# Low parts of weight units: one subtraction in four moved from VectorE to an adding transfer

## The chip, the cores and the metric

The kernel runs on one core of one Trainium2 chip. A core has a matrix engine (PE in the profile, with its weight loads as PEld), a vector engine (DVE), a scalar engine (ACT), a general engine (POOL), and a queue that does nothing here but start transfers (SP). The profile counts 16 DMA engines that carry the transfers. The metric is the device time of one execution in microseconds, as a median of several runs.

## The reference, cut to what matters

The reference is a two-layer decoder trunk over 256 tokens of width 1024. Layer 0 normalises the rows and projects them through one wide input matrix into the columns of a sparse attention, a block attention and a cross-attention into 256 memory tokens. It gates the three outputs and maps them through an output matrix. Layer 1 has the same layout with chunked retention (four heads) and cross-attention again. All weights are float32:

```python
for layer in range(DEPTH):
    if layer % 2 == 0:
        x = even_layer(x, mem_n, cos, sin, *layer_params[layer])
    else:
        x = odd_layer(x, mem_n, rcos, rsin, *layer_params[layer])
return rms_norm(x, final_norm_g)
...
h = rms_norm(x, norm_g)
(...) = _split(h @ w_in, ...)
...
y = jnp.concatenate([...], axis=-1) @ w_out
return x + y
```

What counts here is that almost all of the arithmetic is `h @ w_in`, `mem_n @ w_mem_kv` and `... @ w_out`, with every weight used once.

## The kernel before, in words

**Three products for one.** A float32 product is built from the shorter format float32r. Each operand is written as a sum of a high part (the value rounded to float32r) and a low part (the value minus the high part, again float32r). `mm3` (L133) adds three matmuls into one PSUM bank: high times high (L135), then two with one low part each (L136, L137). All three go into the same bank, one after the other.

**Units of weights.** The host lays the input matrices out as 23 chunks of 512 columns, one chunk of 280 columns, and 14 blocks of the output matrices. A chunk of 512 columns holds 1024 x 512 weights and is used in four units. One unit is 128 x 1024 float32 (512 KB): two of the eight row tiles. `units` (L126) is a generator that yields a chunk's four units: it takes a raw tile that a transfer on SP's queue fills (`load`, L87; tag `raw`, 6 slots), and calls `split` (L118). `split` makes the high part with a copy on ACT (L122, tile `whi`, 3 slots) and the low part with a subtraction on DVE (L123, tile `wlo`, 3 slots). The next step of whatever called `units` is the matmuls of that unit.

**Who uses units.** `project` (L139) has the tokens as stationary operand and the weights as moving operand: 12 matmuls of 128 x 512 for a unit; the first one that needs a low weight is an L136. `project_turned` (L161) has the weights as stationary operand: 24 matmuls of 128 x 256 for a unit, and the first that needs a low weight is an L137, since the operands change places. `project_mem` (L168) is a mixture of both. Chunk `nz` at the start does not go through `units` but calls `split` by half units (L257 to L259). The output projections (L641) call `split` as well, without `units`. So `units` serves 22 chunks of 512 columns (`ksw`, `nq`, `e0`, `mz`, `mk`, `m0`, `mq`, `mv`, `m1`, `e1`, `rq0`, `rk0`, `rv0`, `rz0`, `rv1`, `rz1`, `rq1`, `rk1`, `rv2`, `rz2`, `rv3`, `rz3`, in this order in the program) and the one of 280 columns (in `compress`, L445).

**The rest.** Between the projections stand the attention pieces of layer 0 (`causal_pair`, L358; `mem_attention`, L395) and the retention heads of layer 1 (`ret_head`, L728). They need PE for scores, transposes and outputs, ACT for exponentials and copies, and DVE for reductions and scalings.

**What sets the order.** The program is written in dataflow order. A planner, which plays the program against a time model of its own, gives each engine one fixed order of instructions and adds the semaphores; each queue then runs strictly in that order. Slots of a tag go round: a unit can be written into `whi` or `wlo` once the last matmul that reads the unit three places earlier has ended, and a load can be issued into `raw` once the reader of the unit six places earlier has ended. Matmuls that add into one bank stay in the program's order. POOL has only a few fills of constants before the change: L465, L467, L469 and L518 in the sparse attention's preparation.

Of the kernel before, what the change touches and what calls it, by code (L numbers as in the profile page):

```python
# [10 lines left out]
F32R = mybir.dt.float32r  # L11
I32 = mybir.dt.int32
AF = mybir.ActivationFunctionType
ALU = mybir.AluOpType
AX = mybir.AxisListType

P = 128
# [35 lines left out]
def trunk(  # L53
# [19 lines left out]
    nc = tc.nc  # L73
    sb = ctx.enter_context(tc.tile_pool(name="sb", bufs=1))
    pp = ctx.enter_context(tc.tile_pool(name="pp", bufs=4, space=bass.MemoryType.PSUM))
    V, S, G, PE = nc.vector, nc.scalar, nc.gpsimd, nc.tensor
    count = [0]

    def tl(tag, shape, bufs=1, dt=F32):
        count[0] += 1  # L80
        return sb.tile(shape, dt, tag=tag, bufs=bufs, name=f"{tag}_{count[0]}")
# [5 lines left out]
    def load(t, src):  # L87
        nc.sync.dma_start(t, src)
        return t
# [28 lines left out]
    def split(raw, cols, tag=None):  # L118

        hi = tl(tag or "whi", [P, 1024], NV if tag else 3, F32R)[:, :cols]  # L120
        lo = tl(tag or "wlo", [P, 1024], NV if tag else 3, F32R)[:, :cols]
        S.copy(hi, raw)  # L122
        V.tensor_tensor(lo, raw, hi.bitcast(F32), ALU.subtract)  # L123
        return hi, lo

    def units(src, idx, cols):  # L126

        for u in range(4):
            raw = ahead.pop(0) if ahead else load(tl("raw", [P, 1024], NRAW)[:, : 2 * cols], src[idx + u // 2][:, (u % 2) * 2 * cols : (u % 2 + 1) * 2 * cols])
            wh, wl = split(raw, 2 * cols)  # L130
            yield 2 * u, wh, wl

    def mm3(ps, lh, ll, rh, rl, start, stop, shared=False):  # L133

# [4 lines left out]
    def project(src, idx, lhs, cols=512, tag="pj"):  # L139

        hi, lo = lhs
        ps = [bank(tag) for _ in range(2)]
        for k0, wh, wl in units(src, idx, cols):
            for tok in range(2):
                for j in range(2):
                    kt = k0 + j
                    ts = slice(tok * P, (tok + 1) * P)
                    cs = slice(j * cols, (j + 1) * cols)
                    mm3(ps[tok][:, :cols], hi[:, kt, ts], lo[:, kt, ts], wh[:, cs], wl[:, cs], kt == 0, kt == KT - 1)
        return [p[:, :cols] for p in ps]  # L150
# [10 lines left out]
    def project_turned(src, idx, lhs):  # L161

        ps = [bank("pj") for _ in range(2)]
        for kt, wh, wl in units(src, idx, 512):
            turned_unit(ps, lhs, wh, wl, (kt, kt + 1), range(4))
        return ps

    def project_mem(src, idx, lhs):  # L168

        hi, lo = lhs  # L170
        ps = [bank("pj") for _ in range(2)]
        for k0, wh, wl in units(src, idx, 512):
            turned_unit(ps, lhs, wh, wl, (k0, k0 + 1), range(2))
            for tok in range(2):
                for j in range(2):
                    kt = k0 + j
                    ts = slice(tok * P, (tok + 1) * P)
                    c = slice(j * 512 + 256, j * 512 + 512)
                    mm3(ps[1][:, tok * T : (tok + 1) * T], hi[:, kt, ts], lo[:, kt, ts], wh[:, c], wl[:, c],
                        kt == 0 and tok == 0, kt == KT - 1, True)  # L180
        return ps
# [73 lines left out]
    for q in range(4):  # L255
        gain_split(xraw[q // 2], vect[:, V_G0 : V_G0 + 8], xh, xl, 4 * (q // 2), range(2 * q, 2 * q + 2))
        for j in range(2):  # L257
            wh, wl = split(wraw[q][:, j * 512 : (j + 1) * 512], 512)
# [658 lines left out]
```

## Time and profile before

| | |
|---|---|
| time, median of 3 runs | 444.86 us (444.41 to 445.07) |
| time of the profiled execution | 444.81 us |
| its span, from the first to the last instruction | 443.0 us |
| mean granted TensorE clock | 0.991 |
| instructions | 7033 |
| read from HBM | 72.73 MB |

The times in the prediction are read from one profiled execution. In a row of a group, `x124` is the count of instructions; what stands behind the bar is their busy time in us, the mean length of one in ns, and then the idle time of the engine just before them and what ended it. In a row of the waits, the numbers are the total in us, how often, and the longest. In a row of the timeline the first number is the start in us from the start of the span, the second the length. In a row by windows come the stretch, its length, and for each engine its busy time and its count of instructions, then the granted clock, the share of the DMA engines and GB/s. In a row of transfers the last number is the median time from issue to landing in us.

### The profile page before, as it was taken

The page shows a single profiled execution, that of the slowest core. Times are in us where ns is not written, and L with a number is a line of the kernel's source. Part 1 is how long each engine was busy: PE and PEld are TensorE (multiplying, and loading weights), DVE is VectorE, ACT ScalarE, POOL GpSimd, SP SyncE. Part 2 cuts the span into 40 slices and gives each one's busy share as a digit, 9 for nine tenths or more (in the row PEclk, how much of TensorE's full clock was granted, in tenths as well). Part 3 has the DMA queues.
Part 4 walks back from the last instruction along what each step waited for, and adds up shares of the span by engine and source line. Part 5 has one row for each costly group of instructions (what it writes and reads, how often), then busy time and mean ns, then how long its engine had stood idle before and what let it go on. Part 6 is the DMA issues. An engine that isn't in the chain of part 4 may idle for free.

```text
span 443.0 us, 7033 instructions
## 1 busy us (share of the span) xinstructions
PE 427.0 (96%) x2610; PEld 361.5 (82%) x2610; DVE 308.8 (70%) x712; ACT 245.7 (55%) x445; POOL 1.9 (0%) x9
## 2 busy tenths in 40 slices
PE   8999999999999799999999999999999999999991
PEld 6988999788777567669998988888998888888880
DVE  4997796996576666749668675768777586765415
ACT  5755637776657966737355443754534456445504
POOL 0000000000000000000000000000000000000000
PEclk9999999999999999999999999999999999999996
DMA  8975955753445514343453453664654545765202
GB/s 282 383 248 180 341 168 187 242 169 117 119 132 153 195 55 137 101 131 109 158 188 127 158 165 128 196 197 142 209 169 165 148 171 173 212 212 166 77 0 95
DMA packets 22226, 74.24 MB, mean 168 GB/s; under 512 B 2736, under 2 KB 3504, under 8 KB 22192
## 3 DMA queue, kind: packets, MB, share of 16 engines
q1 hardware_dynamic: 21616, 72.95, 50.1%
q10 hardware_dynamic: 576, 0.84, 0.6%
q8 instruction: 20, 0.33, 0.3%
q14 instruction: 14, 0.11, 0.1%
HBM read 72.73 MB, written 1.05 MB: 167 GB/s over the span
## 4 chain that ended last, share of the span: by engine, by line
PE 95%; DVE 2%; ACT 1%; DMA 1%; issue 0%; ACTq 0%
PE pj L135 24%; PE pj L136 24%; PE pj L137 24%; PE s L100 4%; PE t L194 4%; PE o L100 3%; PE tr L136 1%; PE s L135 1%; PE s L136 1%; PE s L137 1%; PE tr L135 1%; PE tr L137 1%; DMA vec<-in_vec 1%; PE s L732 1%; PE tr L194 1%; DVE v L800 1%
## 5 line engine op out<-in xcount | busy, mean ns | idle before, releaser
L123 DVE TENSOR_TENSOR wlo<-raw,whi 128x1024 fp32r<-128x1024 f32 (+2 forms) x124 | 145.1, 1173 | 72.8 <-ACT whi L122 71.9
L122 ACT CAST whi<-raw 128x1024 fp32r<-128x1024 f32 (+2 forms) x124 | 124.7, 1008 | 96.7 <-PE pj L137 36.8
L136 PE MATMUL pj<-wlo,big 128*128 128x512 f32 (+2 forms) x264 | 99.2, 376 | 0.0
L137 PE MATMUL pj<-whi,big 128*128 128x512 f32 (+2 forms) x264 | 98.4, 373 | 0.0
L135 PE MATMUL pj<-whi,big 128*128 128x512 f32 (+2 forms) x264 | 92.7, 376 | 0.0
L135 PE MATMUL pj<-big,whi 128*128 128x256 f32 x288 | 81.6, 287 | 0.8 <-ACT big L214 0.7
L136 PE MATMUL pj<-big,whi 128*128 128x256 f32 x288 | 81.1, 285 | 0.0
L137 PE MATMUL pj<-big,wlo 128*128 128x256 f32 x288 | 80.6, 286 | 0.0
L136 PEld LDWEIGHTS pj<-wlo,big 128*128 128x128 f32 x264 | 49.7, 188 | 9.7 <-issue 1.0
L135 PEld LDWEIGHTS pj<-big,whi 128*128 128x128 f32 x288 | 54.8, 191 | 2.6 <-ACT big L214 1.1
L137 PEld LDWEIGHTS pj<-whi,big 128*128 128x128 f32 x264 | 49.7, 188 | 8.7 <-issue 0.3
L135 PEld LDWEIGHTS pj<-whi,big 128*128 128x128 f32 x264 | 49.2, 188 | 8.0
L137 PEld LDWEIGHTS pj<-big,wlo 128*128 128x128 f32 x288 | 54.3, 191 | 1.4 <-issue 1.0
L136 PEld LDWEIGHTS pj<-big,whi 128*128 128x128 f32 x288 | 55.0, 191 | 0.4 <-DVE big L215 0.2
L367 ACT ACTIVATE p<-p,mx 128x128 f32<-128x128 f32 (+1 forms) x48 | 21.3, 447 | 3.1 <-DVE mx L365 3.1
L379 ACT COPY pt<-t 128x384 f32<-128x384 f32 x24 | 11.5, 479 | 12.7 <-PE t L194 12.6
L194 PE MATMUL t<-cst,p 128*128 128x128 f32 x104 | 17.9, 282 | 0.6 <-ACT pt L379 0.6
L365 DVE CUSTOM_DVE_ANT_0 p<-s,cst 128x128 f32<-128x128 f32 (+1 forms) x48 | 14.3, 354 | 5.2 <-PE t L194 5.1
L194 PEld LDWEIGHTS t<-cst,p 128*128 128x128 f32 x104 | 11.7, 140 | 6.1 <-issue 3.0
L123 DVE TENSOR_TENSOR v<-raw,v 128x1024 fp32r<-128x1024 f32 x4 | 4.9, 1226 | 14.7 <-PE tr L136 10.9
L135 PE MATMUL pj<-whi,y 128*128 128x512 f32 x36 | 13.4, 408 | 1.0 <-ACT y L387 1.0
L136 PE MATMUL pj<-wlo,y 128*128 128x512 f32 x36 | 14.2, 396 | 0.0
(280 smaller groups left out, 574.0 us busy)
## 6 DMA issues: line engine op xcount, KB each, us to landing
raw<-in_w SPq DMA_DIRECT2D x91, 512.0 KB, 4.0
raw<-in_wout SPq DMA_DIRECT2D x28, 512.0 KB, 3.9
v<-in_xtok SPq DMA_DIRECT2D x4, 512.0 KB, 7.6
raw<-in_w SPq DMA_DIRECT2D x4, 280.0 KB, 3.9
v<-in_w SPq DMA_DIRECT2D x2, 512.0 KB, 5.6
raw<-in_memT SPq DMA_DIRECT2D x2, 512.0 KB, 3.8
raw<-in_memtok SPq DMA_DIRECT2D x2, 512.0 KB, 4.3
v<-in_grow SPq DMA_DIRECT2D x2, 512.0 KB, 7.5
```

The lines of the kernel that those rows point to most:

```text
L100: ins = PE.matmul(out, lhs, rhs, start=start, stop=stop)
L122: S.copy(hi, raw)
L123: V.tensor_tensor(lo, raw, hi.bitcast(F32), ALU.subtract)
L135: PE.matmul(ps, lh, rh, start=start, stop=False, skip_group_check=shared)
L136: PE.matmul(ps, lh, rl, start=False, stop=False, skip_group_check=shared)
L137: PE.matmul(ps, ll, rh, start=False, stop=stop, skip_group_check=shared)
L194: PE.transpose(b[:, i * P : (i + 1) * P], a, ident)
L365: V.tensor_tensor_reduce(p[:, hh, a], ss[hh][tok], cpak[:, C_CAUSAL + a.start : C_CAUSAL + a.stop], -1.0, 3e38, ALU.add, ALU.min, mx[:, hh ...
L367: S.activation(p[:, hh, a], p[:, hh, a], AF.Exp, bias=mx[:, hh, tok : tok + 1], scale=-1.0, accum_out=sm[:, hh, tok : tok + 1])
L379: got = S.copy(pt[:, hh, :384], transposes([p[:, hh, i * P : (i + 1) * P] for i in range(3)]))
L732: PE.matmul(s[:, 0:T], k[:, d, 0:P], q[:, d], start=d == 0, stop=d == 1)
L800: V.tensor_tensor(x0[tok][:, bc], acc[tok][c0 // 512], x0[tok][:, bc], ALU.add)
```

## The change

In `units`, the third of a chunk's four units (`u == 2`) of a chunk with 512 columns gets a different split. ACT makes the high part as before. ACT also writes the negated raw weights, rounded to float32r, into `wlo`; that is the negated high part. Then a transfer, issued on POOL's queue, adds the raw weights to what stands in `wlo`. Its sum is the raw value minus the high part, the low part that DVE computed before. It concerns 22 units, one of each of the 22 chunks; the 280-column chunk, chunk `nz` and the output projections are untouched.

```diff
+    def split_dma(raw):
+
+        hi = tl("whi", [P, 1024], 3, F32R)
+        lo = tl("wlo", [P, 1024], 3, F32R)
+        S.copy(hi, raw)
+        S.activation(lo, raw, AF.Copy, scale=-1.0)
+        nc.gpsimd.dma_start(lo, raw, accum_op=ALU.add)
+        return hi, lo
+
     def units(src, idx, cols):
 
         for u in range(4):
             raw = ahead.pop(0) if ahead else load(tl("raw", [P, 1024], NRAW)[:, : 2 * cols], src[idx + u // 2][:, (u % 2) * 2 * cols : (u % 2 + 1) * 2 * cols])
-            wh, wl = split(raw, 2 * cols)
-            yield 2 * u, wh, wl
+            if u == 2 and cols == 512:
+                yield 2 * u, *split_dma(raw)
+            else:
+                yield 2 * u, *split(raw, 2 * cols)
```

## The prediction

> **What bounds the kernel now.** I read the head of the page first, then the chain that ended last, then the table by windows.
>
> ```profile
> span 443.0 us, 7033 instructions
> PE 427.0 (96%) x2610; PEld 361.5 (82%) x2610; DVE 308.8 (70%) x712; ACT 245.7 (55%) x445; POOL 1.9 (0%) x9
> ...
> PE 95%; DVE 2%; ACT 1%; DMA 1%; issue 0%; ACTq 0%
> ```
>
> PE is busy for 427.0 of 443.0 us and holds 95% of the chain. By stages (the first number behind the stretch is its length, the second PE's busy time):
>
> ```profile
> 16.00:62.00 46.00, 46.00 (x317) 41.87 (x316) 39.52 (x86) 27.57 (x38) 0.31 (x1) 1.00 0.70 251
> 62.00:196.00 134.00, 130.03 (x853) 101.14 (x849) 94.10 (x289) 90.11 (x226) 0.53 (x1) 1.00 0.47 148
> 196.00:256.00 60.00, 59.92 (x469) 56.01 (x470) 44.92 (x78) 31.48 (x56) 0.00 (x0) 1.00 0.45 149
> 256.00:382.00 126.00, 126.00 (x665) 108.30 (x665) 91.02 (x192) 61.34 (x72) 0.00 (x0) 1.00 0.54 172
> ```
>
> PE has no hole from 16 to 62 us nor from 196 to 382 us, even where DVE is busy for 39.52 of 46 us; the attention of layer 0 (62 to 196 us) leaves 3.97 us. So what can shorten the kernel is only what PE waits for. The waits say whether that is DVE:
>
> ```profile
> DVE wlo L123 <- ACT whi L122: 71.9, 65, 4.2
> ACT whi L122 <- PE pj L137: 36.8, 34, 3.2
> ...
> PE o L100 <- ACT pt L379: 1.8, 1, 1.8
> ...
> PEld pj L136 <- DVE wlo L123: 0.3, 1, 0.3
> ...
> PEld pj L137 <- DVE wlo L123: 0.2, 1, 0.2
> ```
>
> PE's weight loads waited for a low part twice, 0.5 us in all. It is the other way round: ACT's high parts wait for PE to free a slot, and DVE's low parts wait for ACT. DVE runs ahead of the bound.
>
> **What is removed.** For 22 units, one subtraction on DVE.
>
> ```profile
> L122 ACT CAST whi<-raw x124: 602/1047/1075, 4.5 to 416.6; 128x1024 fp32r<-128x1024 f32 x112, 128x512 fp32r<-128x512 f32 x8, 128x560 fp32r<-128x560 f32 x4
> L123 DVE TENSOR_TENSOR wlo<-raw,whi x124: 683/1225/1227, 5.1 to 417.7; 128x1024 fp32r<-128x1024 f32 x112, 128x512 fp32r<-128x512 f32 x8, 128x560 fp32r<-128x560 f32 x4
> ...
> L268 ACT ACTIVATE raw<-raw x2: 1060/1060/1060, 74.8 to 77.7; 128x1024 f32<-128x1024 f32 x2
> ...
> DMA to landing us min/median/max: 2.8/4.1/8.5
> ```
>
> (Durations in ns: least, median, most; the last row is of the loads into `raw`.) That is 22 x 1.225 = 27.0 us off DVE. It is worth the 0.5 us of waits above at most, and I count 0: those waits belong to any of 124 units, of which 22 change.
>
> **What is added.** Per unit, one activation on ACT and one transfer.
>
> ```profile
> L777 ACT ACTIVATE v<-pj,rstd 128x512 f32<-128x512 f32 x8 | 5.5, 688 | 8.7 <-PE pj L137 8.7
> ```
>
> The low part existed 1.05 us (ACT) plus 1.23 us (DVE) after ACT began the unit. Now it exists after two ACT passes and a landing. The nearest row for the second pass is the 128x1024 activation of L268, 1.06 us, so 2.1 us for both. The bounds are 1.0 us, since the rounding copy of the same shape takes that, and 1.4 us, if it went by twice a 128x512 activation (L777, 0.69 us).
>
> ```profile
> q1 hardware_dynamic: 21616, 72.95, 50.1%
> ```
>
> No row shows an adding transfer, nor any transfer from POOL's queue. It moves the shape of a `raw` load (128x1024 f32, 512 KB) and has to read two tiles where a load reads one. A median load lands after 4.1 us. Queue q1 kept 16 engines busy for 50.1% of 443.0 us, 222 us, to move 72.95 MB; another 0.524 MB so costs 1.6 us. I take 4.1 + 1.6 = **5.7 us**. The low end is 2.8 us, the shortest load (adding and second read free); the high end is 8.5 + 1.6 = 10.1 us, the longest load with the second read. With 2.1 us before it, the low part is there 7.8 us after ACT begins the unit, 5.5 us later than before.
>
> [...]
>
> **How much of it is hidden.** Between ACT's start on a unit and PE's first matmul with its low part lies the time that hides the new path; it cannot grow, as ACT starts when PE frees one of three slots. The first, the fifteenth and the last of the 22 units, each with ACT's start and that matmul:
>
> ```profile
> 21.68 1.05 ACT L122 CAST whi<-raw 128x1024 fp32r<-128x1024 f32 x1
> ...
> 24.98 0.39 PE L136 MATMUL s<-wlo,big 128*128 128x512 f32 x1
> ...
> 282.58 1.04 ACT L122 CAST whi<-raw 128x1024 fp32r<-128x1024 f32 x1
> ...
> 287.00 0.61 PE L135 MATMUL pj<-whi,big 128*128 128x512 f32 x2
> 287.46 0.39 PE L136 MATMUL pj<-wlo,big 128*128 128x512 f32 x1
> ...
> 369.38 1.04 ACT L122 CAST whi<-raw 128x1024 fp32r<-128x1024 f32 x1
> ...
> 375.93 0.40 PE L136 MATMUL pj<-wlo,big 128*128 128x512 f32 x1
> ```
>
> These are 3.3, 4.9 and 6.5 us. Read the same way in the timeline, the 22 units have, in program order (us): ksw 3.3, nq 6.2, e0 6.4, mz 9.3, mk 5.4, m0 11.0, mq 8.0, mv 9.3, m1 7.0, e1 5.5, rq0 7.2, rk0 7.9, rv0 7.0, rz0 6.5, rv1 4.9, rz1 6.5, rq1 5.1, rk1 6.0, rv2 7.1, rz2 6.5, rv3 4.9, rz3 6.5. What falls short of 7.8 us is a hole on PE: 4.5, 1.6, 1.4, 2.4, 0.8, 2.3, 0.6, 0.8, 1.3, 2.9, 1.3, 2.7, 1.8, 0.7, 1.3, 2.9, 1.3 = **30.6 us in 17 units**; five units (mz, m0, mq, mv, rk0) are covered. Nothing gives the time back: the next chunk's unit again waits for its slot.
>
> What PE can do meanwhile: products of high parts (L135) that do not need the low part, as many as there are banks, two for a unit. In some units both already go ahead (287.00 above, x2); for about ten the second is new, 0.23 us each, -2.3 us. In the attention stage other matmuls are ready: I take half of mk's 2.4 us off, -1.2 us.
>
> **Queues.** POOL's queue is in order and has two fills that wait long:
>
> ```profile
> 55.29 0.31 POOL L467 MEMSET yf<- 64x256 f32 x1 [53.73 <-PE o L457]
> 63.37 0.53 POOL L518 MEMSET tmp<- 128x512 f32 x1 [7.77 <-PE s L100]
> ```
>
> ```profile
> 48.92 1.04 ACT L122 CAST whi<-raw 128x1024 fp32r<-128x1024 f32 x1
> ...
> 55.25 0.40 PE L137 MATMUL pj<-big,wlo 128*128 128x256 f32 x2
> ```
>
> A transfer queued behind the first fill would not start before 55.6 us. For e0's unit (ACT starts at 48.92 us, low part needed by the second of the two L137, at 55.4 us) that is a hole of up to 5.9 us instead of 1.4, once. I count 0, as the planner places instructions by when they become ready, and e0's does some 4 us earlier. On ACT the new passes are 22 x 1.06 = 23 us, 55% to 61% busy. ACT's casts already wait for PE (36.8 us above), so in the projections they fit. The raw slot is held 5.5 us longer, and loads queued behind on SP shift with it; the cover is six slots:
>
> ```profile
> ACT whi L122 <- DMA raw<-in_w: 1.7, 2, 1.3
> ```
>
> ACT waited for loads 1.7 us in the whole kernel; without that cover each of the 22 would cost up to 5.5 us, so I keep 0. DMA engines gain 22 x 2 x 1.6 = 70 us at most of 16 engines' 443, from 50% to 66%.
>
> ```profile
> L378 DVE TENSOR_SCALAR p<-p,sm 128x128 f32<-128x128 f32 (+1 forms) x36 | 9.9, 312 | 0.4
> ```
>
> [...]
>
> **The sum**, against the profiled execution: 30.6 - 2.3 - 1.2 = +27.1 us on 444.8 us, **472 us**. The profiled 444.81 us stands 0.05 us below the median of the three runs, 444.86 us.
>
> **The rivals.**
>
> *Slow transfer.* An add costs more than a second read, or the queue's start is slow: 7 us and above. At 8.5 us the low part is there after 10.6 us, 21 units fall short, by 86 us; with -5 us for L135 that is +81 us, 526 us. Then PE's holes also meet the clock that is granted to it:
>
> ```profile
> 432.97 0.28 PE L137 MATMUL s<-v,y 128*128 128x256 f32 x1
> ```
>
> ```profile
> 431.60:435.10 3.50, 1.65 (x10) 1.22 (x8) 3.22 (x6) 1.98 (x7) 0.00 (x0) 1.00 0.00 0
> 435.20:441.00 5.80, 0.00 (x0) 0.00 (x0) 3.21 (x11) 2.71 (x8) 0.00 (x0) 0.50 0.42 155
> ```
>
> The granted clock fell from 1.00 to 0.50 within some 2 us of the last matmul's end at 433.25. A hole of 3 us or more may so be followed by a stretch at half speed; if that lasts as long as the hole, 14 holes cost up to 25 us more. For it: contention at the start (a load took 8.5 us). Against: the steady stages load one unit at a time.
>
> *Short transfer.* 3 to 4.6 us. At 4.0 us the low part comes after 6.1 us, seven units fall short by 7.6 us in all, less 1.5 us for L135: +6 us, 451 us. For it: the shortest load, 2.8 us.
>
> *Not slower.* One mechanism: the landing takes under 3 us, so only ksw falls short, by some 1.6 us, and the relief of DVE reaches PE in the attention stage, whose 3.97 us of idle PE end behind chains through DVE and ACT (the 1.8 us of L100 above). Five of the 22 units lie there, 5 x 1.23 = 6.1 us off DVE; if that took away 3 us of the 3.97, the result were 443.4 us. It decides at a landing of about 3 us; above 3.5 us the holes (4.5 us) outweigh all that PE could gain. Against it: ACT gets 5.3 us more in that same stage.
>
> **How the numbers follow.** My forecast, a landing between 4.6 and 7 us, gives about 455 to 496 us: 0.58. Slow transfer, above 496 us: 0.20. Short transfer, 446 to 455 us: 0.14. Not slower: 0.08, of it 0.05 faster and 0.03 the same. About 0.2% (0.9 us) is what a measurement can tell from no change. So faster 0.05, same 0.03, slower 0.92. The range is 448 to 518 us: it leaves out the not-slower case, the edge of the short one, and the half of the slow one above 8 us of landing, together under 0.2.
>
> **What would show it.** The profile after should have 22 transfers from POOL's queue with a median landing near 5.7 us; a wait of PE's L136 or L137 on that transfer, some 27 us in about 17 pieces, longest in ksw and in rv1 and rv3, none in m0 and mv; DVE down by 27 us, ACT up by 23 us, PE's own busy time the same. It is wrong if the transfer lands in under 4 or over 7 us, if the planner has moved whole matmul groups into the holes, or if PE's clock falls below 1.00 in mid-kernel.

## The result, and the profile after

The changed kernel takes **460.84 us** (median of 4 runs, 456.94 to 464.9); the kernel before, beside it on the same chip, 444.97 us (444.41 to 447.35). The ratio is 1.0313, 95% interval 1.0263 to 1.0364. The four runs of the changed kernel differ in the clock that was granted to them: spans of 455.1, 456.5, 461.5 and 463.0 us at mean clocks of 0.989, 0.987, 0.977 and 0.973; a run that is over 1.5% above the fastest of its kernel, here the one of 463.0 us, is left out of the ratios. The profiled execution took 458.31 us with a span of 456.5 us, 13.5 us more than the 443.0 us of before; the parts below add up to these 13.5 us.

The new function moves the lines: the cast of a unit with the new path is L130, its negation L131, its transfer L132, the three matmuls are L146, L147 and L148 (L135 to L137 before). The head of the page and the chain of work that ended last:

```profile
span 456.5 us, 7093 instructions
...
PE 432.0 (95%) x2610; PEld 363.5 (80%) x2610; DVE 285.9 (63%) x690; ACT 264.7 (58%) x467; POOL 20.9 (5%) x31
...
PE 68%; issue 13%; DMA 12%; ACT 3%; DVE 3%; POOL 0%; ACTq 0%; POOLq 0%
...
wlo<-raw POOLq DMA_DIRECT2D x22, 512.0 KB, 5.1
```

PE's share of the chain fell from 95% to 68%, and DMA has 12% of it: the bound now passes through transfers. The 13% of issue stand ahead of transfers (14.48 us of them before mk's at 86.45 us) while PE is at work, so the fall of PE's share does not measure the loss. The last row is that of the 22 new transfers, with their median landing. PE's busy time rose by 5.0 us, and its idle time by 8.5. By stages, in the table by windows:

```profile
16.00:62.00 46.00, 42.74 (x249) 37.50 (x248) 32.89 (x77) 28.06 (x39) 3.03 (x4) 0.96 0.82 268
62.00:196.00 134.00, 128.87 (x868) 101.48 (x867) 89.84 (x284) 92.15 (x226) 4.83 (x6) 0.99 0.55 167
196.00:256.00 60.00, 58.42 (x439) 52.60 (x438) 37.97 (x72) 35.23 (x62) 3.44 (x4) 1.00 0.59 167
256.00:382.00 126.00, 123.74 (x682) 106.59 (x681) 77.90 (x166) 67.25 (x78) 7.75 (x9) 1.00 0.70 205
```

The first stage had no hole before; now PE is idle for 3.26 of 46 us, and its clock is below 1.00 (0.96). The last two stages, where PE was idle for 0.08 us before, now have 1.58 and 2.26 us of idle PE. The waits of PE for low parts, in the table of waits:

```profile
PEld pj L147 <- DMA wlo<-raw: 4.7, 4, 2.4
...
PE pj L147 <- DMA wlo<-raw: 3.6, 3, 2.1
...
PEld pj L148 <- DMA wlo<-raw: 2.4, 4, 0.8
...
PE pj L148 <- DMA wlo<-raw: 1.5, 3, 0.6
PE pj L147 <- DVE wlo L123: 1.5, 1, 1.5
```

PE's own waits for the transfer come to 3.6 + 1.5 = 5.1 us in six pieces, not to 27 us in seventeen. Where the rest of the loss arises is seen when the end of each chunk's matmuls is compared in the two timelines. The delay grew by (us): ksw 5.0, e0 3.2, mk 3.1, the first output projection 1.1, e1 0.3, rq0 0.7, rv0 1.4, rv1 0.4, rk1 0.9, rv3 0.7, and 0.2 or less elsewhere; it shrank by 2.1 in mz, 0.8 in m0, 0.4 ahead of ksw and 0.3 in nq. The 3.2 in e0 and the 2.1 in mz belong together: 64 matmuls of the compressed scores (L100, 2.06 us from 65.67 us) now stand inside e0, where they stood behind it before, and at the end of mz both kernels have done the same matmuls. Together e0 and mz cost 1.1 us. At the end of mv, the last projection of layer 0, it was 7.7 us. The largest piece, ksw, in the timeline of PE and ACT:

```profile
21.37 1.03 ACT L130 CAST whi<-raw 128x1024 fp32r<-128x1024 f32 x1
...
22.31 1.06 ACT L131 ACTIVATE wlo<-raw 128x1024 fp32r<-128x1024 f32 x1
...
23.68 1.00 POOL L132 DMA_DIRECT2D wlo<-raw  x1 [22.11 <-ACT wlo L131]
...
26.02 0.51 PE L146 MATMUL pj<-whi,big 128*128 128x512 f32 x1 [0.87 <-ACT whi L122]
...
28.02 0.50 PE L147 MATMUL pj<-wlo,big 128*128 128x512 f32 x1 [1.50 <-DVE wlo L123]
...
29.01 0.63 PE L147 MATMUL pj<-wlo,big 128*128 128x512 f32 x1
```

The low part of ksw's third unit landed at 29.70 us, 8.3 us after its cast began. PE did not wait for it there: the new order puts matmuls of the next chunk, nq (bank `pj`), ahead of ksw's remaining ones (bank `s`). But nq's operands were not ready either, and PE waited 0.87 us for a cast and 1.50 us for a subtraction by DVE. Then the clock fell; the table by windows shows the 3.4 us before and the 3.4 us at the lower clock:

```profile
25.18:28.58 3.40, 1.06 (x3) 0.67 (x4) 3.40 (x9) 2.07 (x2) 0.00 (x0) 1.00 1.05 266
28.59:32.00 3.41, 3.41 (x10) 2.62 (x9) 1.87 (x3) 1.23 (x2) 0.00 (x0) 0.50 0.82 250
151.47:154.87 3.40, 1.64 (x14) 0.98 (x13) 1.23 (x2) 2.96 (x8) 0.00 (x0) 1.00 0.77 210
154.89:158.29 3.40, 3.40 (x16) 2.21 (x16) 1.84 (x7) 2.15 (x7) 0.00 (x0) 0.50 0.99 390
```

In mid-kernel the granted clock was 0.50 twice for 3.41 us. In the first one the 128x512 matmuls start 0.43 us apart (29.01, 29.43, 29.86 us), right behind it 0.23 us (32.00, 32.23, 32.47 us). I count half of PE's work as lost in each such stretch, 1.7 us, an estimate from the clock of 0.50. The second one is not shown to be the change's: the hole of 1.76 us ahead of it, where an output matmul (L100) waits for a copy on ACT, stands in the kernel before as well (at 146.27 us), and the clock did not fall there (rows in the last section). So of the 13.5 us, 5.4 are holes that end with a transfer's landing (all holes in the timeline, short ones too), 2.8 are holes that end with a cast or a subtraction (2.4 of them at ksw), 3.4 are the two stretches at half clock, and 1.9 us are left, nearly all in PE's busy time at full clock.

### The profile page after: what moved, and what is told of

Same layout as the page of the kernel before. It is cut to its first block, busy times and chain, and to the rows that moved or that the text cites. A ratio compares the mean times of both kernels' runs of the same rounds, so it can differ in the third digit from the quotient of the medians.

```text
span 456.5 us, 7093 instructions
## 1 busy us (share of the span) xinstructions
PE 432.0 (95%) x2610; PEld 363.5 (80%) x2610; DVE 285.9 (63%) x690; ACT 264.7 (58%) x467; POOL 20.9 (5%) x31
## 4 chain that ended last, share of the span: by engine, by line
PE 68%; issue 13%; DMA 12%; ACT 3%; DVE 3%; POOL 0%; ACTq 0%; POOLq 0%
PE pj L147 17%; PE pj L148 16%; PE pj L146 16%; DMA wlo<-raw 8%; PE t L205 4%; PE s L100 3%; PE o L100 3%; DMA raw<-in_xT 2%; DMA v<-in_xtok 2%; PE tr L147 1%; PE tr L146 1%; DVE wlo L123 1%; PE tr L148 1%; ACT whi L122 1%; PE s L147 1%
## 5 line engine op out<-in xcount | busy, mean ns | idle before, releaser
L123 DVE TENSOR_TENSOR wlo<-raw,whi 128x1024 fp32r<-128x1024 f32 (+2 forms) x102 | 118.3, 1162 | 88.1 <-ACT whi L122 87.4
L122 ACT CAST whi<-raw 128x1024 fp32r<-128x1024 f32 (+2 forms) x102 | 101.6, 999 | 92.9 <-PE pj L148 40.9
L147 PE MATMUL pj<-wlo,big 128*128 128x512 f32 (+2 forms) x264 | 100.1, 380 | 5.3 <-DMA wlo<-raw 3.6
L148 PE MATMUL pj<-whi,big 128*128 128x512 f32 (+2 forms) x264 | 98.6, 375 | 0.0
L146 PE MATMUL pj<-whi,big 128*128 128x512 f32 (+2 forms) x264 | 92.7, 379 | 0.9 <-ACT whi L122 0.9
L146 PE MATMUL pj<-big,whi 128*128 128x256 f32 x288 | 81.6, 287 | 1.4 <-ACT big L225 0.9
L148 PE MATMUL pj<-big,wlo 128*128 128x256 f32 x288 | 79.8, 287 | 1.6 <-DMA wlo<-raw 1.5
L147 PE MATMUL pj<-big,whi 128*128 128x256 f32 x288 | 80.9, 284 | 0.0
L147 PEld LDWEIGHTS pj<-wlo,big 128*128 128x128 f32 x264 | 50.1, 190 | 15.5 <-DMA wlo<-raw 4.7
L146 PEld LDWEIGHTS pj<-whi,big 128*128 128x128 f32 x264 | 49.8, 189 | 10.1 <-ACT whi L122 1.1
L146 PEld LDWEIGHTS pj<-big,whi 128*128 128x128 f32 x288 | 54.9, 191 | 3.6 <-ACT big L225 1.3
L148 PEld LDWEIGHTS pj<-whi,big 128*128 128x128 f32 x264 | 50.1, 190 | 8.4
L148 PEld LDWEIGHTS pj<-big,wlo 128*128 128x128 f32 x288 | 53.9, 191 | 3.3 <-DMA wlo<-raw 2.4
L147 PEld LDWEIGHTS pj<-big,whi 128*128 128x128 f32 x288 | 55.0, 191 | 0.7 <-issue 0.3
L132 POOL DMA_DIRECT2D wlo<-raw x22 | 19.1, 867 | 350.3 <-ACT wlo L131 277.3
L131 ACT ACTIVATE wlo<-raw 128x1024 fp32r<-128x1024 f32 x22 | 23.3, 1058 | 9.2 <-PE pj L147 5.1
L130 ACT CAST whi<-raw 128x1024 fp32r<-128x1024 f32 x22 | 22.9, 1041 | 7.1 <-PE pj L147 6.3
```

What stands on the lines that cost most here:

```text
L131: S.activation(lo, raw, AF.Copy, scale=-1.0)
L132: nc.gpsimd.dma_start(lo, raw, accum_op=ALU.add)
L146: PE.matmul(ps, lh, rh, start=start, stop=False, skip_group_check=shared)
L147: PE.matmul(ps, lh, rl, start=False, stop=False, skip_group_check=shared)
L148: PE.matmul(ps, ll, rh, start=False, stop=stop, skip_group_check=shared)
```

## The experiments

Two theories stood against each other. **The landing** (L in the expectations): time is lost where a unit's cover is shorter than the path of negation and transfer. **The work** (W): the passes on ACT and the transfers cost by themselves, by their place in the queues and the order that the planner makes. Every edit is to the changed kernel unless it says otherwise. Experiments 1, 2, 5, 8 and 12 let two small tiles share their space (`sc` and `ctr`), to make room.

**1. The path beside the kernel.** Negation and transfer go into a tile that nothing reads; PE's low part comes from DVE.

```diff
-        S.activation(lo, raw, AF.Copy, scale=-1.0)
-        nc.gpsimd.dma_start(lo, raw, accum_op=ALU.add)
+        aside = tl("aside", [P, 1024], 1, F32R)
+        S.activation(aside, raw, AF.Copy, scale=-1.0)
+        nc.gpsimd.dma_start(aside, raw, accum_op=ALU.add)
+        V.tensor_tensor(lo, raw, hi.bitcast(F32), ALU.subtract)
```

> The 22 units keep the second ACT pass and the adding transfer, but both go into a tile of their own that nothing reads; PE's low part comes from the DVE subtraction as before the change. Theory L (PE waits for the landing of the transfer, and the holes lower its clock): 445 to 447 us, no wait of PE on a transfer. Theory W (the added work itself costs: 23 us on ACT, the traffic, raw slots held longer): 456 to 464 us, as with the change.

Measured: 455.75 us (454.86 to 457.54), ratio 1.0246 (1.0214 to 1.0278). That seems to speak for the work. But the table of waits shows a wait that the changed kernel does not have:

```profile
ACT aside L132 <- DMA raw<-in_w: 52.2, 20, 4.4
```

The tile beside is always free, so the planner put the negation early in ACT's order, ahead of its load. ACT then stood 52.2 us waiting for loads, with other work queued behind it. The experiment had made a new cost of its own, so it decided nothing; experiment 5 repeats it without that.

**2. Four slots instead of three** for the high and low parts (in `split` and `split_dma`; one raw slot fewer, for space). ACT can start a unit earlier, so the cover grows.

```diff
-NRAW = 6
+NRAW = 5
...
-        hi = tl("whi", [P, 1024], 3, F32R)
-        lo = tl("wlo", [P, 1024], 3, F32R)
+        hi = tl("whi", [P, 1024], 4, F32R)
+        lo = tl("wlo", [P, 1024], 4, F32R)
```

> The change, with four slots instead of three for high and low parts (one raw slot fewer pays for it: five instead of six). ACT can start a unit one unit (2.7 us or more) earlier. Theory L: the landing is covered in all units but perhaps ksw, 445 to 449 us, PE's holes on the transfer under 1 us. Theory W: 456 us or more, since ACT's passes and the traffic are all there and a raw slot is missing.

Measured: 457.11 us (454.49 to 460.04), ratio 1.0278 (1.0235 to 1.0322). The median misses the landing theory and lies in the range of the work; the place of the loss speaks for the landing. At the end of the first output projection it is 9.3 us behind and at its own end 9.7 us, so layer 1 loses next to nothing. Its rows by windows, first stage and last:

```profile
16.00:62.00 46.00, 42.17 (x244) 36.77 (x243) 32.68 (x80) 28.13 (x40) 3.04 (x4) 0.96 0.83 272
```

```profile
256.00:382.00 126.00, 126.00 (x695) 109.28 (x694) 76.89 (x167) 69.24 (x80) 8.62 (x10) 1.00 0.75 216
```

With a fourth slot the 2.26 us of holes in the last stage are gone. The start is not helped: PE is idle for 3.83 us there, and a stretch at half clock follows again. ACT now begins so early that it stands before loads (2.6 us in the changed kernel, 3.6 us in experiment 8, which has these slots without the new path):

```profile
ACT whi L122 <- DMA raw<-in_w: 8.1, 6, 2.2
```

**3. The negation reads the high part**, so that it can't stand ahead of the cast. The arithmetic is the same.

```diff
-        S.activation(lo, raw, AF.Copy, scale=-1.0)
+        S.activation(lo, hi.bitcast(F32), AF.Copy, scale=-1.0)
```

> The change, but ACT negates the high part instead of the raw weights (the same values), so the negation can't run before the cast of the unit. With the change it ran before it in 14 of 22 units. Theory L: in those the low part comes 1.9 to 2.5 us later; five of them had no slack (e0, e1, rv1, rq1, rv3), three had 0.4 to 1.7 us, so the holes grow by 11 to 15 us: 468 to 478 us. Theory W: the work is the same, 456 to 464 us.

Measured: 477.13 us (476.67 to 479.46), ratio 1.0732 (1.0699 to 1.0766). Nothing is added; only an order is forbidden, and 16.3 us more are lost. The waits:

```profile
PE pj L147 <- DMA wlo<-raw: 12.3, 6, 4.6
...
PE pj L148 <- DMA wlo<-raw: 4.5, 3, 2.4
```

These are 16.8 us, 11.7 us more than in the changed kernel. Experiment 3 shows that PE's loss follows the moment at which the transfer can start, and what the planner's freedom to negate first was worth.

**4. DVE adds the raw weights** to the negated high part, in place of the transfer: ACT's 22 extra passes alone.

```diff
-        nc.gpsimd.dma_start(lo, raw, accum_op=ALU.add)
+        V.tensor_tensor(lo, raw, lo.bitcast(F32), ALU.add)
```

> The change, but DVE adds the raw weights to the negated high part, in the transfer's place. ACT has its 22 second passes, DVE is as busy as before the change, no transfer is added. Theory L: the low part comes 1.2 us instead of 5.1 us after the negation, 445 to 447 us. If ACT's 23 us are the cost: 452 us or more.

Measured: 448.06 us (446.57 to 451.28), ratio 1.007 (1.0046 to 1.0094). The passes cost some 3 us, a little more than the landing theory had put them at. All of it arises before the end of mv. PE is idle for 15.9 us there and for 16.0 us in the kernel before, so the loss is not in holes. Most of the profiled run's 2.0 us lies in the score matmuls of 64 rows: each takes about as long (363 ns, 356 before), but they overlap less, and their busy time is 1.9 us more. First the kernel before, then this one:

```profile
L100 PE MATMUL s<-s,v 64*128 64x128 f32 (+1 forms) x64 | 8.6, 356 | 0.0
```

```profile
L100 PE MATMUL s<-s,v 64*128 64x128 f32 (+1 forms) x64 | 10.5, 363 | 0.0
```

**5. The first experiment again, with the negation read from the high part.**

```diff
-        S.activation(aside, raw, AF.Copy, scale=-1.0)
+        S.activation(aside, hi.bitcast(F32), AF.Copy, scale=-1.0)
```

> As the first experiment (pass and transfer into a tile that nobody reads, DVE makes the low part that PE reads), but the negation reads the high part, so that it can't stand ahead of a late load in ACT's order. Theory L (the time is lost where PE waits for the transfer's landing): only the ACT passes are left, 446 to 449 us, as the 448.06 us of the fourth experiment. Theory W (the passes and transfers cost by the order and the load they make, whoever reads the result): 454 us or more, as the first experiment's 455.75 us. The chain of waits shows no ACT wait on a raw load under L.

Measured: 447.56 us (446.3 to 450.68), ratio 1.0051 (1.0021 to 1.0082). The same passes, the same transfers, the same landings (median 4.6 us), and 13 us of the loss are gone as soon as PE needs none of them. The waits of ACT for loads are down to one:

```profile
ACT whi L122 <- DMA raw<-in_w: 1.4, 1, 1.4
```

With experiment 4 this settles it between the two theories: about 3 us of the 16 are the work, the rest is waiting for the landing and what follows from it, the planner's other order and the fallen clock included, which no run separates. The third term, contention of the 22 transfers with loads, is in the 2.7 us of this run too.

**6 and 7. Layer 0 alone, layer 1 alone.**

```diff
-            if u == 2 and cols == 512:
+            if u == 2 and cols == 512 and idx < W["e1"]:
```

(and `idx >= W["e1"]` in the seventh.)

> The new path for the eight chunks of layer 0 (ksw to mv) alone. The changed kernel was 7.7 us behind at the end of mv and 13.5 us at its own end. If the loss is local to each unit: 451 to 454 us. If the loss of layer 1 is only what an early delay leaves behind (loads and slots that never catch up): 457 to 460 us, as with all 22.

> The new path for the fourteen chunks from e1 to rz3 alone. If each short unit of layer 1 costs its own wait for the landing: 5 to 7 us, 450 to 452 us, and PE waits on the transfer stand in the profile. If layer 1's loss only follows from the early delay: 445 to 447 us and no such waits.

Measured: layer 0 alone 457.44 us (453.53 to 462.96), ratio 1.0256 (1.0204 to 1.0308); layer 1 alone 447.17 us (446.65 to 451.62), ratio 1.0058 (1.0032 to 1.0084). The sixth's median lies where it should by the theory of what an early delay leaves behind, its profiled run (453.53 us) where it should by local loss. The profile decides: the delay is 8.7 us at the end of mv and 8.8 us at the end of the kernel, so nothing grows in layer 1. Its runs spread with the granted clock (0.986 to 0.968). The seventh's 2.3 us are less than half of the 5 to 7 us expected if each short unit costs its own wait, but such waits are there. Its row by windows for the last stage, and its waits:

```profile
256.00:382.00 126.00, 124.89 (x656) 106.69 (x655) 79.12 (x179) 68.77 (x81) 8.59 (x10) 1.00 0.70 207
```

```profile
PEld pj L147 <- DMA wlo<-raw: 1.2, 3, 0.5
...
PEld pj L148 <- DMA wlo<-raw: 1.0, 2, 0.8
```

Layer 1, for which I had summed 20.7 us of holes, costs 2.3 us by itself.

**8. A control for the second**: the kernel before, with its four slots and five raw slots (`NRAW = 5`, `whi` and `wlo` with 4).

> A control for the second experiment: the kernel before, with its four slots each for the high and low parts, its five raw slots and its shared tile, and no change of the split. If the second experiment's loss at the start (6 to 10 us) came from the raw slot that it gave up: 450 us or more here. If it came from the new path: 444 to 447 us.

Measured: 446.54 us (445.69 to 447.12), ratio 1.0025 (1.0005 to 1.0045). The slots cost 1.1 us (0.2 to 2.0), so most of the loss in the second experiment (9.3 us up to the first output projection) is that of the new path.

**9 and 10. Three chunks, and all but these three.**

```diff
-            if u == 2 and cols == 512:
+            if u == 2 and cols == 512 and idx in [W[n] for n in ("ksw", "e0", "mk")]:
```

(and `not in` in the tenth.)

> The new path in three chunks alone: ksw, e0 and mk, behind which the changed kernel's delay grew by 4.6, 3.2 and 3.1 us. If the loss is local to the units whose cover is short at the start and in the attention stage: 452 to 457 us. If it is spread over all 22: 446 to 448 us.

> The complement of the ninth experiment: the new path in the other nineteen chunks. If the loss is local: second layer alone cost 2.3 us, and the five chunks left of the first layer are covered but for nq (about 1 us), so 446.5 to 449.5 us. If it is spread: 455 to 459 us.

Measured: three chunks 453.68 us (450.96 to 454.99), ratio 1.0162 (1.0118 to 1.0207); the other nineteen 449.47 us (447.98 to 452.65), ratio 1.0104 (1.005 to 1.0158). Three of 22 units carry 8.3 us, nineteen carry 4.1 us; together 12.5 of the 15.9 us between the medians. In the ninth's timeline of PE, the holes at ksw (the 1.50) and mk, and behind mk's the clock again:

```profile
27.80 0.55 PE L147 MATMUL pj<-wlo,big 128*128 128x512 f32 x1 [1.50 <-DVE wlo L123]
...
92.56 0.50 PE L147 MATMUL pj<-wlo,big 128*128 128x512 f32 x1 [2.40 <-DMA wlo<-raw]
```

```profile
89.56:92.96 3.40, 1.00 (x10) 0.56 (x7) 3.15 (x17) 2.73 (x5) 0.00 (x0) 1.00 0.55 105
92.97:96.38 3.41, 3.41 (x10) 2.67 (x9) 2.90 (x13) 1.37 (x6) 0.00 (x0) 0.50 0.74 250
```

**11. The nine best covered chunks** (7.0 us of cover or more in the kernel before): the condition lists mz, m0, mq, mv, m1, rq0, rk0, rv0 and rv2.

> The new path in the nine chunks whose cover in the kernel before is 7.0 us or more (mz, m0, mq, mv, m1, rq0, rk0, rv0, rv2). With two passes of 2.1 us and the measured landing of 5.1 us, the low part comes after 7.2 us; what falls short is some 0.6 us in all. Cover theory: 444.5 to 446 us. If the ninth part of POOL's transfers or the ACT passes cost by themselves: 447 us or more.

Measured: 447.92 us (446.55 to 450.52), ratio 1.0049 (1.0022 to 1.0077). A miss: the cover hides the landing (one hole of 0.20 us ends with a transfer), but the kernel is still some 2 us slower. Of the profiled run's 1.9 us, 1.3 arise by the end of m0. Experiments 4 and 5 show the same kind of loss with no transfer in PE's way at all, so even a hidden transfer is not free here. Whether ACT's pass costs this or the other order that the planner makes with it, these runs do not separate: 1.1 us of the loss arise in mk, which does not have the new path here.

**12. A plain copy instead of an adding transfer.** DVE makes the low part in a tile of its own, POOL's queue copies it.

```diff
-        S.activation(lo, raw, AF.Copy, scale=-1.0)
-        nc.gpsimd.dma_start(lo, raw, accum_op=ALU.add)
+        aside = tl("aside", [P, 1024], 1, F32R)
+        V.tensor_tensor(aside, raw, hi.bitcast(F32), ALU.subtract)
+        nc.gpsimd.dma_start(lo, aside)
```

> What the adding costs in the landing: DVE makes the low part in a tile of its own, and POOL's queue copies it into the tile that PE reads, without adding. If the second read and the add cost (my 1.6 us of 5.7): median landing 3.3 to 3.8 us instead of 5.1. If the queue's way is what takes the time and the add is nearly free: 4.5 to 5.0 us. The path is one pass on ACT (1.05 us), one on DVE (1.23 us) and the landing, and it can't begin before the cast; with a landing near 4.8 us the time should be near the third experiment's 477 us, with 3.5 us near 460 us.

Measured: 478.47 us (475.92 to 479.6), ratio 1.072 (1.0667 to 1.0773). The transfers' row, first of this kernel and then of the changed one:

```profile
DMA to landing us min/median/max: 4.6/4.9/6.6
```

```profile
DMA to landing us min/median/max: 4.5/5.1/8.0
```

Adding was nearly free here: the plain copy lands as late, after 4.9 us against 5.1 at the median. The time is that of experiment 3, and the shape of the path too: nothing can start before the cast.

## Why the prediction came out as it did, point by point

The time forecast (472 us) and the sign were right, and the time lies within the forecast's own 455 to 496 us. The mechanism is the forecast's: cover against landing, shown by experiments 3 and 5. But the sum of 27.1 us stood against 13.5, and the prediction's own signs of that sum (27 us of waits in 17 pieces, no clock below 1.00, no matmul groups moved) did not come out. Two things that it had named as signs of being wrong did come: matmuls have moved into the holes (nq's into ksw, 64 compressed scores into e0), and the clock fell in mid-kernel. Of the 13.5 us only 5.4 are holes of the kind that the sum is made of; 3.4 us of clock and 2.8 us of other waits, which it did not have, brought the time nearer to 472 us. That part is luck. Step by step:

**Nothing comes off the bound with DVE.** Right. The group of L123 before, and after:

```profile
L123 DVE TENSOR_TENSOR wlo<-raw,whi 128x1024 fp32r<-128x1024 f32 (+2 forms) x124 | 145.1, 1173 | 72.8 <-ACT whi L122 71.9
```

```profile
L123 DVE TENSOR_TENSOR wlo<-raw,whi 128x1024 fp32r<-128x1024 f32 (+2 forms) x102 | 118.3, 1162 | 88.1 <-ACT whi L122 87.4
```

That is 26.8 us less, and PE gained nothing from it in any stage. (In the head rows, where overlapping instructions count once, DVE is down by 22.9 us and ACT up by 19.0 us.)

**Two passes on ACT, 2.1 us.** Right in length, 1.06 us a pass:

```profile
L131 ACT ACTIVATE wlo<-raw 128x1024 fp32r<-128x1024 f32 x22 | 23.3, 1058 | 9.2 <-PE pj L147 5.1
...
L132 POOL DMA_DIRECT2D wlo<-raw x22 | 19.1, 867 | 350.3 <-ACT wlo L131 277.3
```

**The landing of 5.7 us**, as a load's 4.1 and 1.6 for a second read. It is 5.1 us, 4.5 at the least, and POOL begins the transfer some 0.3 us after the negation's end. The size was near, the parts were wrong: experiment 12 shows no cost of the second read (least landings of 4.6 us for the copy and 4.5 us for the add), and the least landing through POOL's queue is 4.5 us where that of a 512 KB load in the kernel before was 3.1 us (the 2.8 us are those of a load of 280 KB).

**The cover "cannot grow, as ACT starts when PE frees one of three slots".** This is the step that failed. In nine of the thirteen units of layer 1 on which I had counted a hole, and in 14 of the 22 in all, ACT negates first and casts later. For rv1, in the timeline of the changed kernel:

```profile
293.07 1.06 ACT L131 ACTIVATE wlo<-raw 128x1024 fp32r<-128x1024 f32 x1
...
294.43 0.86 POOL L132 DMA_DIRECT2D wlo<-raw  x1 [13.56 <-ACT wlo L131]
...
294.61 1.04 ACT L130 CAST whi<-raw 128x1024 fp32r<-128x1024 f32 x1
...
299.51 0.50 PE L147 MATMUL pj<-wlo,big 128*128 128x512 f32 x1
```

The negation reads only the raw weights and needs only a `wlo` slot. The slot comes from the unit three places earlier, the last one of the chunk before. Where that chunk has the weights as moving operand, its `wlo` is read last by an L147 and its `whi` by an L148, later; behind chunks with stationary weights (rq0, rk0, rv0, rk1, rv2) the cast does come first. So in rv1 the path began 1.5 us ahead of the cast, and only one pass stood before the transfer: 6.4 us from the negation's start to the landing, 4.9 us from the cast's. I had put 7.8 us against a cover of 4.9; the new cover is 6.4 us and the path is as long. Experiment 3 takes that freedom away: there the same unit is

```profile
301.40 1.05 ACT L130 CAST whi<-raw 128x1024 fp32r<-128x1024 f32 x1
...
303.68 1.07 ACT L131 ACTIVATE wlo<-whi 128x1024 fp32r<-128x1024 f32 x1
...
305.04 0.86 POOL L132 DMA_DIRECT2D wlo<-raw  x1 [14.76 <-DVE p L747]
```

```profile
309.86 0.79 PE L147 MATMUL pj<-wlo,big 128*128 128x512 f32 x1 [2.26 <-DMA wlo<-raw]
```

with a hole of 2.26 us (my list had 2.9). The two numbers are near partly by chance: two other passes on ACT (L766) stand between the cast and the negation, 1.2 us that my sum did not have, and the landing took 4.8 us instead of 5.7.

From the end of the first output projection on, this kernel loses 16.2 us: 10.5 in six holes that end with a transfer and 3.4 by 6.8 us at half clock, with 2.3 left. I had summed 20.7 us in thirteen units there; the changed kernel lost 4.6. So even in the order that I assumed the list is too long, for a second reason: the cover also grows where PE has other work. For rz0, one of four units (rz0 to rz3) with 1.3 us each in my list and no hole here:

```profile
286.98 1.04 ACT L130 CAST whi<-raw 128x1024 fp32r<-128x1024 f32 x1
```

```profile
293.69 0.39 PE L147 MATMUL o<-v,pt 128*128 128x512 f32 x1
...
295.32 0.40 PE L147 MATMUL pj<-wlo,big 128*128 128x512 f32 x1
```

Seven matmuls of the retention heads now stand ahead of the first one with the low part, and the cover from the cast is 8.3 us where it was 6.5 (7.4 in the changed kernel).

**Layer 0.** I had ksw 4.5, nq 1.6, e0 1.4, and mk 2.4 with 1.2 off: 8.7 us. The delay at the end of mv is 7.7 us. That agrees for partly wrong reasons, so by luck. At ksw PE does not wait for the transfer but runs into nq's unready operands, and 1.7 us of the loss are the clock. At e0 and mk the transfers took 6.9 and 8.0 us, with four loads or more in flight during them. "Nothing gives the time back" holds but for 0.8 us in m0; the 2.1 us of mz are work that was done in e0.

**More high products ahead.** Right: ahead of the first matmul with a low weight PE does four with the high weights instead of two or three in e1, rq0, rk0, rq1 and rk1, and six in e0.

**Queues.** Right to count nothing for POOL's fills (the transfer of e0 began at 54.20 us, 0.3 us after its negation) and for the raw slots:

```profile
ACT whi L122 <- DMA raw<-in_w: 2.6, 2, 1.5
```

That is 1.7 us before and 2.6 us now. Wrong for ACT: its passes "fit" in the projections but cost 2 to 3 us in layer 0 (experiments 4, 5 and 11). In experiment 4 most of it is in the score matmuls; in 5 and 11 these take 8.8 and 9.1 us, and the chain there is open. Issuing a transfer took POOL 0.86 us, in ksw 1.00 us.

**The rivals.** The slow transfer did not come, but its side effect did: the clock fell after holes of 1.50 us (ksw), 1.76 us (at 153.96 us) and 2.40 us (mk in experiment 9), not only of 3 us. (At a landing of 8.5 us, 17 units of my list fall short by 3 us or more, not 14; the forecast does not hang on it.) The short transfer's range (446 to 455 us) was missed by 3 us in the profiled run, though its 7.6 us of holes in all are nearer to the 5.4 us in the trace than my 30.6. Nothing of "not slower" showed: no attention stage gained.

What stays open: 1.9 us of the 13.5 in PE's busy time at full clock, and the 3.4 us between the medians by which three and nineteen chunks do not sum to all 22; stretches at half clock, which differ from run to run, are as large as that.

## What to carry to other kernels

Before work is moved to a transfer, measure for each place the time between the first moment at which its inputs and its slot are there and the consumer's first need, and set it against the whole path: here one pass of 1.06 us, 0.3 us, and a landing of 4.5 to 8.0 us. Look at which operand the new step really depends on: here reading the raw tile instead of the rounded one was worth 16 us, as it let the path begin before the cast. And taking work off an engine that runs ahead of the bound brings nothing, while the engine that takes it over may pay.

## What the runs showed of the hardware

- A 512 KB transfer from SBUF to SBUF through POOL's queue landed after 4.5 us at the least when it adds and after 4.6 us as a plain copy (experiment 12). The adding one kept POOL for 0.86 us to issue, the copy for 0.53 us. In the changed kernel four of the five that landed in under 4.6 us had at most one load in flight beside them (the fifth had two, of which one landed 0.2 us after its start), and the two longest (6.9 us in e0, 8.0 us in mk) four or more. In between the number of loads does not set the order: rv0's took 6.0 us beside one load, rv1's 5.0 us beside two.
- In mid-kernel the granted clock fell to 0.50 for 3.41 us at a time: at 28.59 and 154.89 us in the changed kernel, at 28.12 and 92.97 us in the ninth experiment. In the 3.40 us just ahead PE had worked for 1.06 us (ksw) and 1.64 us (from 151.47 us), and for 1.32 and 1.00 us in the ninth experiment. As little work was not always followed by half clock. The kernel before has the hole of 1.76 us too, with 1.64 us of work in 3.40 us, and the changed kernel one of 2.12 us at mk, with 1.28 us of work; the clock stayed at 1.00 behind both. What decides it is not shown. The rows of the kernel before, then those of the changed one at mk:

```profile
143.80:147.20 3.40, 1.64 (x14) 1.00 (x13) 1.25 (x2) 2.98 (x8) 0.00 (x0) 1.00 0.91 270
147.20:150.60 3.40, 2.73 (x20) 1.76 (x22) 2.79 (x14) 2.99 (x11) 0.00 (x0) 1.00 0.90 341
```

```profile
91.10:94.50 3.40, 1.28 (x12) 0.71 (x10) 3.40 (x12) 3.07 (x8) 0.00 (x0) 1.00 0.71 214
94.50:97.90 3.40, 3.40 (x16) 2.86 (x17) 1.43 (x11) 1.48 (x5) 0.00 (x0) 1.00 0.57 204
```
